# Queries' latent columns among the key products, the norm's shift added at the reload, the next weights split behind the queries: a change to a two-layer trunk kernel

## The chip, the cores and the metric

The kernel runs on one core of a Trainium2 chip. The metric is the time of one execution on the device in microseconds (us); several executions are timed and the median is taken. A smaller number is better. Times of the trace are counted from the start of its span.

## The reference

The program is a small trunk of two layers over 256 latent rows and 256 context rows of 1024 features, in float32. Layer 0 mixes with a bidirectional chunked mLSTM, layer 1 with multi-head latent attention; a gated ConvFFN follows each mixer. The change lies in layer 1's attention, which the reference computes like this (cut):

```python
def _mla_q(h, w_dq, q_norm, w_uq, ang):
    q = (_rms_norm(h @ w_dq, q_norm) @ w_uq).reshape(B, T, A_HEADS, A_DNOPE + A_DROPE)
    q_nope, q_rope = jnp.split(q, [A_DNOPE], axis=-1)
    return jnp.concatenate([q_nope, _axial_rope(q_rope, ang[0][:, None], ang[1][:, None])], -1)

def _mla_kv(h, w_dkv, kv_norm, w_ukv, ang):
    ckv, k_rope = jnp.split(h @ w_dkv, [A_KVLORA], axis=-1)
    k_rope = _axial_rope(k_rope, ang[0], ang[1])
    kv = (_rms_norm(ckv, kv_norm) @ w_ukv).reshape(B, T, A_HEADS, A_DNOPE + A_DV)
    ...

yl = _blocked_attend(ql, k_all, v_all).reshape(B, T, -1) @ w_out
x  = _layer_norm(ALPHA * x + ml[2] * yl, ln_g[i, 0], ln_b[i, 0])
```

There are 8 heads; keys and values are the 256 context rows and the 256 latent rows, queries are the latent rows alone. The residual `x` that goes into the last line is the output of layer 0's second norm: normalised rows times a gain `ln_g` plus a shift `ln_b` over the 1024 features.

## The kernel before, in words

**Precision.** Each float32 operand of a product is split into a high and a low part: ACT casts to the matmul type (high), DVE subtracts (low). A product is then three matmuls: high x high, high x low, low x high (`mm3`, lines 395 to 397). A tile with two parts is a "u" tile; there are 31 of them. Weights go through the class `Stream`: SP's queue loads a raw block of up to 1024 columns (line 299), ACT casts it (L334) and DVE subtracts (L337). The parts of a "wide" block go into two u tiles, those of others into one of three "w" tiles (`NB`). `use` splits ahead as far as `limit` allows, `pump(limit)` splits up to an index of the planned order without using anything. A raw block's buffer is loaded again when its split has been done.

**The order.** The kernel is written as a program for a scheduler that builds one in-order list for each engine: TensorE (PE), VectorE (DVE), ScalarE (ACT), GpSimd (POOL), and SP's queue. It may put an instruction ahead of others of the program if its operands and buffers allow it by its own account. `issue_after(i)` keeps what is issued under it behind the instruction `i`.

**Around the change**, in order of time (the function `mla`, line 1690 onwards):

- `dkv_mm`, and the four `dq` steps: latent columns of keys and values, and of the queries.
- `ln_x` (L1273), run in the background: it multiplies the layer-0 rows `z` by the gain (L1282), adds the shift (L1283) and stores them to DRAM as `x2d` (L1284, POOL's queue). Gain and shift rows (`gr`, `br`) are loaded by `bcast` (L1143).
- `rms` (L1574 to L1577) makes the normalised latent columns `cq` of the queries.
- `ukn(1)` (L1636): products `kn` of all 8 heads' keys for the latent rows, 48 matmuls of 256 columns.
- `cqT`: six PE transposes of `cq` (L1719), scaled and split (L1721, L1722).
- `qr`: the rotary parts of all queries (weights `uqr`), then `uv`: the values `v`; then rotation, scaling and split of `qr` into `qrs` (L1585 to L1587, L1747, L1748).
- `queries(i)`: the other part `qn` of the queries of heads 2i and 2i+1 (three weight blocks `uqn`, used from heads 0, 2 and 5 on), split at L1767 and L1768.
- `rotary(i)`: transposes `qrT` of two heads' rotary parts (L1776) and their copy (L1779).
- Then a loop over the heads h: transposes `PT` of the probabilities of head h-2 (L1810) with their split, `scores(h)` (products `s`, L1791 for the rotary part; maximum L1793; exp L1795; reciprocal L1796; multiply L1797 on the probabilities `P`), `attend(h-2)` (products `o`, split into `oT`). In it, `st.pump(ao + h)` splits weight blocks for what follows; `ao` is the index of the first `uqn` block, the eight `aout` blocks (output product) come three later, then the blocks of the next FFN (`fin1`).
- `res_load` (L1321) loads the residual rows from `x2d` into four tiles `xres` on POOL's queue; `bcast` loads the gate. `outmm("aout", ...)` makes the output product `y`, and `ln_rows` (L1148) the gated residual (L1157, L1158) and its norm.

Of the kernel before, what the change touches and what calls it, by code (L numbers as in the profile page):

```python
# [10 lines left out]
AF = mybir.ActivationFunctionType  # L11
ALU = mybir.AluOpType
# [15 lines left out]
H1 = 8  # L28
# [7 lines left out]
SUMS = 5  # L36

IDLE = 5

AHEAD = 8  # L40
QA, QB, QC = 2, 4, 6
# [324 lines left out]
class K:  # L366
# [866 lines left out]
    def ln_T4(self, zs, A, B, dst):  # L1233
# [6 lines left out]
        for t in range(2):  # L1240
# [5 lines left out]
            if not t:  # L1246
                for _ in range(IDLE):
                    pin(nc.tensor.matmul(idle, w[:, 0:128], w[:, 0:512], start=True, stop=True))
# [20 lines left out]
            if k % 2:  # L1269
                yield  # L1270

    def ln_x(self, ln, zs, dst):


        nc = self.nc
        g = self.bcast(self.a["ln_g"][ln:ln + 1, :], "gr")
        b = self.bcast(self.a["ln_b"][ln:ln + 1, :], "br")
        yield
        for t in range(2):
            for h in range(2):  # L1280
                c = slice(h * 512, (h + 1) * 512)
                nc.vector.tensor_tensor(zs[t][:, c], zs[t][:, c], g[h], op=ALU.mult)  # L1282
                nc.vector.tensor_tensor(zs[t][:, c], zs[t][:, c], b[h], op=ALU.add)  # L1283
                nc.gpsimd.dma_start(dst[t][:, c], zs[t][:, c])  # L1284
                yield

# [28 lines left out]
            r.append([(self.ps("y")[:, 0:b - a], slice(a, b)) for a, b in zip(cuts, cuts[1:])])  # L1315
        return r

    def res_load(self, src, t0):
        xs = []
        for t in range(2):  # L1320
            hs = []  # L1321
            for h in range(2):
                x = self.s2("xres")
                self.nc.gpsimd.dma_start(x, src[t0 + t][:, h * 512:(h + 1) * 512])
                hs.append(x)
            xs.append(hs)
        return xs
# [305 lines left out]
                nc.scalar.copy(self.krT[:, 0, cs], p)  # L1633
                nc.vector.tensor_sub(self.krT[0:64, 1, cs], p[0:64], self.krT[0:64, 0, cs])

    def ukn(self, g):  # L1636

        cs = slice(g * 256, (g + 1) * 256)
        for h in range(H1):
            w = self.wk[h // 4]  # L1640
            if h % 2 == 0:
                ps = self.ps("kn")
            hs = slice((h % 2) * 256, (h % 2 + 1) * 256)
            for k in range(2):
                c = slice((h % 4) * 256 + k * 128, (h % 4) * 256 + (k + 1) * 128)
                self.mm3(ps[:, hs], (w[0][:, c], w[1][:, c]), (self.ckT[k][:, 0, cs], self.ckT[k][:, 1, cs]),
                         k == 0, k == 1)
            if h % 2:
                for j in range(2):
                    u = self.kn[h - 1 + j]  # L1650
                    self.split(u[:, 0, cs], u[:, 1, cs], ps[:, j * 256:(j + 1) * 256])
# [36 lines left out]
    def mla(self, hl):  # L1688
        nc, st = self.nc, self.st
# [6 lines left out]
        for c in range(4):  # L1696
            w = st.use(("dq", 0, c))
            self.tick()
            for kk in range(2):
                k = 2 * c + kk  # L1700
# [8 lines left out]
        for t in range(2):  # L1709
            r = self.s2("cq")  # L1710
            self.rms(pss[t][:, 0:384], 384, r[:, 0:384])
            cq.append(r)
        self.ukn(1)
        g = self.smc("qng")
        cqT = []
        for k in range(3):
            pt = self.ps("cqT")
            for t in range(2):
                nc.tensor.transpose(pt[:, t * 128:(t + 1) * 128], cq[t][:, k * 128:(k + 1) * 128], self.ident)  # L1719
            u = self.hf("cqT")  # L1720
            nc.scalar.activation(u[:, 0], pt[:, 0:256], AF.Copy, scale=g[:, k:k + 1])  # L1721
            nc.vector.scalar_tensor_tensor(u[:, 1], pt[:, 0:256], g[:, k:k + 1], u[:, 0],  # L1722
                                           op0=ALU.mult, op1=ALU.subtract)
            cqT.append(u)
        pss = [self.ps("qr0"), self.ps("qr1")]
        for c in range(2):
            w = st.use(("uqr", 0, c))
            for kk in range(2 - c):
                k = 2 * c + kk
# [9 lines left out]
        scale = float((DN + DR) ** -0.5)  # L1739

        qr = []
        for t in range(2):
            r = self.s2("qr")
            self.rope_rows(r, pss[t], t, 512)
            u = self.pool.tile([128, H1, 2, 64], F32R, tag="u", name="qrs", bufs=NU)
# [8 lines left out]
        def queries(i):  # L1754

            ps = self.ps("qn")
            for h in (2 * i, 2 * i + 1):
                hs = slice((h % 2) * 256, (h % 2 + 1) * 256)
                for k in range(3):
                    b = h * 3 + k  # L1760
                    if b % 8 == 0:
                        wq[0] = st.use(("uqn", 0, b // 8))
                    c = slice((b % 8) * 128, (b % 8 + 1) * 128)
                    self.mm3(ps[:, hs], (wq[0][0][:, c], wq[0][1][:, c]), (cqT[k][:, 0], cqT[k][:, 1]),
                             k == 0, k == 2)
            u = self.u("qn")
            nc.scalar.activation(u[:, 0], ps, AF.Copy, scale=scale)  # L1767
            nc.vector.scalar_tensor_tensor(u[:, 1], ps, scale, u[:, 0], op0=ALU.mult, op1=ALU.subtract)  # L1768
            qn.append(u)

        def rotary(i):

            pt = self.ps("qrT")
            for j in range(2):
                for t in range(2):
                    nc.tensor.transpose(pt[:, j * 256 + t * 128:j * 256 + (t + 1) * 128],  # L1776
                                        qr[t][:, 2 * i + j].rearrange("p a b -> p (a b)").bitcast(F32), self.ident)
            u = self.pool.tile([128, 512], F32R, tag="s2", name="qrT", bufs=NS)
            nc.scalar.copy(u, pt)  # L1779
            qrT.append(u)  # L1780
# [3 lines left out]
        def scores(h):  # L1784
            Ps = []
            for t in range(2):
                ps = self.ps("s1")
                c = slice((h % 2) * 256 + t * 128, (h % 2) * 256 + (t + 1) * 128)
                self.mm3(ps, (qn[h // 2][:, 0, c], qn[h // 2][:, 1, c]), (kn[h][:, 0], kn[h][:, 1]), True, False)
                for x in range(2):  # L1790
                    nc.tensor.matmul(ps, qrT[h // 2][:, c], krT[:, x], start=False, stop=x == 1)  # L1791
                mx, sm = self.tiny(1, "mx"), self.tiny(1, "sm1")
                nc.vector.tensor_reduce(mx, ps, axis=AX.X, op=ALU.max, negate=True)  # L1793
                P = self.s2("P1")
                nc.scalar.activation(P, ps, AF.Exp, bias=mx, scale=1.0, accum_out=sm)  # L1795
                nc.vector.reciprocal(sm, sm)  # L1796
                nc.vector.tensor_scalar(P, P, sm, None, op0=ALU.mult)  # L1797
                Ps.append(P)
            return Ps
# [3 lines left out]
        def trans(h, Ps):  # L1803
            PT = []
            for i in range(2):
                pt = self.ps("PT1")
                for j in range(2):
                    s = 2 * i + j
                    for t in range(2):
                        nc.tensor.transpose(pt[:, j * 256 + t * 128:j * 256 + (t + 1) * 128],  # L1810
                                            Ps[t][:, s * 128:(s + 1) * 128], self.ident)
                u = self.u("PT1")
                self.split(u[:, 0], u[:, 1], pt)
                PT.append(u)
            return PT
# [11 lines left out]
            oc = slice((h % 2) * 256, (h % 2 + 1) * 256)  # L1827
            self.split(oT[-1][:, 0, oc], oT[-1][:, 1, oc], ps[:, 0:256])

        ao = st.nu  # L1830
        Ps, PTs = {}, {}
        queries(0)
        queries(1)
        rotary(0)
        for h in range(H1 + 1):
            if 1 <= h < H1:
                st.pump(ao + h)
            if h >= 2:
                PTs[h - 2] = trans(h - 2, Ps.pop(h - 2))
            if h < H1:  # L1840
                Ps[h] = scores(h)
            if h < 6 and h % 2 == 1:
                rotary(h // 2 + 1)
            if h < 2:
                queries(h + 2)
            if h >= 2:
                attend(h - 2, PTs.pop(h - 2))
        yield oT
# [6 lines left out]
def build(tc, off, a, out):  # L1855
    es = ExitStack()
    with es:
        k = K(tc, es, off, a)
        nc = k.nc
# [44 lines left out]
        xr = k.res_load(tokr, 0)  # L1904
# [19 lines left out]
        xr = k.res_load(tokr, 2)  # L1924
# [20 lines left out]
        x2d = k.dr.tile([2, 128, D], F32, name="x2d")  # L1945
# [5 lines left out]
        def mid(g, zs, stats, first=None):  # L1951
            if g is None:
                st.limit = kv0 + PA
                k.rope_load()
                k.mla_ctx(hc)
                return
            return norm1(g, zs, stats, first)

        def norm1(g, zs, stats, first):
            A, B = k.ln_mod_cols(1, 1, 0, 1 - g)  # L1960
            if first is not None:
                first()
                hlu.extend([k.u("hl") for _ in range(4)])
            yield from k.z_norm(zs, stats)
            yield from k.ln_T(zs, A, B, hl if g else hc, g == 1, False)
            if g:
                k.late.append(k.ln_x(1, zs, [x2d[0], x2d[1]]))
        k.w_fout0(x1d, mid)
        hc = hcu = None
        k.tick(1)  # L1970
# [11 lines left out]
        hl = hlu = None  # L1982
        o1 = lambda i: (oT[i // 2][:, 0, (i % 2) * 256:(i % 2 + 1) * 256],
                        oT[i // 2][:, 1, (i % 2) * 256:(i % 2 + 1) * 256])
        xr = k.res_load(x2d, 0)
        gate = k.bcast(k.gd[1, 2][0:1, :], "gate")
        pl = k.acc4(True)
        k.outmm("aout", range(8 - TAIL["aout"]), o1, pl, 0, 8, 1)
# [21 lines left out]
        xr = k.res_load(x3d, 0)  # L2010
        gate = k.bcast(k.gd[1, 5][0:1, :], "gate")
        gr = k.bcast(a["ln_g"][3:4, :], "gr")
        br = k.bcast(a["ln_b"][3:4, :], "br")
# [23 lines left out]
```

## Time and profile before

| what | value |
|---|---|
| median of 3 runs | 1361.63 us (1359.55 to 1362.25) |
| the profiled execution's own time | 1359.2 us |
| its span | 1357.4 us |
| granted TensorE clock, mean | 0.999 |
| instructions on PE / DVE / ACT / POOL | 6663 / 1731 / 1236 / 216 |
| HBM read, written | 263.03 MB, 33.46 MB |

The profile comes from one execution that took 1359.2 us; it shows 1357.4 us of it as its span, and the rest lies around it. In a row of a timeline the first number is the start in us, the second the duration in us, then engine, line and operation, what is written and read, the shape and a count; in brackets at the end the idle time of the engine before it and who ended it. In a list of waits the numbers are us in total, times, and the longest. Rows of the chain of waits give start, length, engine and line. PE's matmuls overlap each other: a row may last 0.39 us while the next one starts 0.23 us after it.

### The profile page before, as it was taken

The page shows a single profiled execution, that of the slowest core. Times are in us where ns is not written, and L with a number is a line of the kernel's source. Part 1 is how long each engine was busy: PE and PEld are TensorE (multiplying, and loading weights), DVE is VectorE, ACT ScalarE, POOL GpSimd, SP SyncE. Part 2 cuts the span into 40 slices and gives each one's busy share as a digit, 9 for nine tenths or more (in the row PEclk, how much of TensorE's full clock was granted, in tenths as well). Part 3 has the DMA queues.
Part 4 walks back from the last instruction along what each step waited for, and adds up shares of the span by engine and source line. Part 5 has one row for each costly group of instructions (what it writes and reads, how often), then busy time and mean ns, then how long its engine had stood idle before and what let it go on. Part 6 is the DMA issues. An engine that isn't in the chain of part 4 may idle for free.

```text
span 1357.4 us, 18736 instructions
## 1 busy us (share of the span) xinstructions
PE 1342.4 (99%) x6663; PEld 1120.6 (83%) x6663; DVE 1056.4 (78%) x1731; ACT 711.9 (52%) x1236; POOL 122.1 (9%) x216
## 2 busy tenths in 40 slices
PE   9999999999999999999999999999999999999997
PEld 6777888888888888888898888888888888888886
DVE  4787756677688697897979878667898889888873
ACT  4764544445734545464644334334557767466660
POOL 0122000011101011030001000000001000000100
PEclk9999999999999999999999999999999999999999
DMA  9887848789676374785727877646997436366750
GB/s 368 315 271 269 294 162 245 235 289 304 215 250 194 98 246 142 239 297 190 232 92 250 295 234 236 213 148 215 309 279 220 140 102 223 104 192 188 256 194 31
DMA packets 92078, 297.73 MB, mean 219 GB/s; under 512 B 12073, under 2 KB 16425, under 8 KB 91985
## 3 DMA queue, kind: packets, MB, share of 16 engines
q1 hardware_dynamic: 62848, 218.65, 48.7%
q0 software_dynamic: 17472, 57.57, 13.6%
q10 hardware_dynamic: 11664, 20.32, 4.2%
q8 instruction: 52, 0.85, 0.3%
q14 instruction: 42, 0.34, 0.1%
HBM read 263.03 MB, written 33.46 MB: 218 GB/s over the span
## 4 chain that ended last, share of the span: by engine, by line
PE 93%; DMA 3%; DVE 2%; ACT 1%; issue 1%; ACTq 0%; SPq 0%; DVEq 0%
PE fin L1374 8%; PE y L396 6%; PE y L397 6%; PE y L395 6%; PE fin L395 6%; PE fin L396 6%; PE fin L397 6%; PE tok L395 6%; PE tok L396 6%; PE tok L397 6%; PE qk L395 4%; PE qk L397 4%; PE qk L396 4%; DMA adaw<-in_ada 2%; PE up L395 2%; PE up L397 1%
## 5 line engine op out<-in xcount | busy, mean ns | idle before, releaser
L337 DVE TENSOR_TENSOR w<-raw,w 128x1024 fp32r<-128x1024 f32 (+2 forms) x286 | 343.8, 1204 | 140.0 <-ACT w L334 139.2
L334 ACT CAST w<-raw 128x1024 fp32r<-128x1024 f32 (+2 forms) x286 | 297.2, 1039 | 290.8 <-PE tok L397 78.4
L500 DVE SCALAR_TENSOR_TENSOR junk<-ar,bc 128x1024 f32<-128x1024 f32 x128 | 156.2, 1220 | 4.0 <-ACT bc L542 1.4
L396 PE MATMUL fin<-h,w 128*128 128x512 f32 (+1 forms) x376 | 141.2, 376 | 0.0
L397 PE MATMUL fin<-h,w 128*128 128x512 f32 (+1 forms) x376 | 140.9, 375 | 0.0
L395 PE MATMUL fin<-h,w 128*128 128x512 f32 (+1 forms) x376 | 140.8, 376 | 0.1
L1374 PE MATMUL fin<-h,w 128*128 128x256 f32 (+1 forms) x640 | 111.9, 337 | 0.0
L1374 PEld LDWEIGHTS fin<-h,w 128*128 128x128 f32 x640 | 98.3, 190 | 13.4
L395 PE MATMUL qk<-xc,w 128*128 128x512 f32 x256 | 100.6, 393 | 0.0
L397 PE MATMUL qk<-xc,w 128*128 128x512 f32 x256 | 99.9, 390 | 0.0
L396 PE MATMUL qk<-xc,w 128*128 128x512 f32 x256 | 99.8, 390 | 0.0
L396 PEld LDWEIGHTS fin<-h,w 128*128 128x128 f32 x376 | 70.8, 188 | 12.9 <-DVE h L1228 0.2
L397 PEld LDWEIGHTS fin<-h,w 128*128 128x128 f32 x376 | 70.8, 188 | 12.9
L395 PEld LDWEIGHTS fin<-h,w 128*128 128x128 f32 x376 | 70.5, 188 | 13.1 <-ACT h L1227 0.3
L397 PEld LDWEIGHTS qk<-xc,w 128*128 128x128 f32 x256 | 48.1, 188 | 9.8
L396 PEld LDWEIGHTS qk<-xc,w 128*128 128x128 f32 x256 | 48.1, 188 | 9.7
L395 PEld LDWEIGHTS qk<-xc,w 128*128 128x128 f32 x256 | 48.1, 188 | 9.7
L395 PE MATMUL tok<-w,hT 128*128 128x512 f32 x128 | 49.9, 390 | 0.0
L397 PE MATMUL tok<-w,hT 128*128 128x512 f32 x128 | 49.8, 389 | 0.0
L396 PE MATMUL tok<-w,hT 128*128 128x512 f32 x128 | 49.8, 389 | 0.0
L681 ACT ACTIVATE fg<-fg 128x512 f32<-128x512 f32 (+1 forms) x44 | 23.2, 527 | 46.1 <-DVE fg L679 39.9
L337 DVE TENSOR_TENSOR wu<-raw,wu 128x1024 fp32r<-128x1024 f32 (+1 forms) x37 | 43.7, 1204 | 4.1 <-ACT wu L334 3.9
(470 smaller groups left out, 3142.3 us busy)
## 6 DMA issues: line engine op xcount, KB each, us to landing
raw<-in_ws SPq DMA_DIRECT2D x282, 512.0 KB, 4.6
ar<-in_adaT SPq DMA_DIRECT2D x80, 512.0 KB, 4.6
adaw<-in_ada SPq DMA_DIRECT2D x16, 512.0 KB, 8.0
t2d<-raw ACTq DMA_DIRECT2D x13, 512.0 KB, 4.8
raw<-t2d SPq DMA_DIRECT2D x13, 512.0 KB, 6.6
raw<-in_ws POOLq DMA_DIRECT2D x13, 512.0 KB, 7.9
zr<-fd ACTq DMA_DIRECT2D x33, 128.0 KB, 4.6
xmd<-xr POOLq DMA_DIRECT2D x16, 256.0 KB, 4.8
```

Source lines behind the costliest of these rows:

```text
L334: k.nc.scalar.copy(h[:, :cols], src)
L337: k.nc.vector.tensor_sub(l[:, :cols], src, h[:, :cols])
L395: mm(out, w[0], x[0], start=start, stop=False, skip_group_check=on)
L396: mm(out, w[0], x[1], start=False, stop=False, skip_group_check=on)
L397: mm(out, w[1], x[0], start=False, stop=stop, skip_group_check=on)
L500: nc.vector.scalar_tensor_tensor(o, w, 1.0, self.bc[j], op0=ALU.mult, op1=ALU.mult, accum_out=col[:, k, j:j + 1])
L681: nc.scalar.activation(tmp[:, :n], tmp[:, :n], AF.Silu)
L1374: nc.tensor.matmul(ps[:, :n] if x else ps, w[x][:, c], hT(k)[0] if x else both(k), start=i == 0, stop=i == 15)
```

## The change

1. `ln_x` gets a parameter `shift`. For the rows of layer 0's second norm it is False: neither are the shift's rows loaded nor are they added by DVE; what is stored is rows times gain. At the reload, `res_load` gets the shift's row as `base`: it first fills each residual tile with the shift (a transfer that repeats one row over all partitions), and a second transfer of POOL's queue adds the stored rows to it.
2. `ukn` takes a range of heads. The key products of heads 0 to 5 (`QH = 6`) come before the transposes of `cq`, those of heads 6 and 7 behind them.
3. In the attention, `limit` is set to the third `uqn` block before the queries, so that it isn't split by them; it is split by a pump behind the split of the second pair of queries (`issue_after` both of its instructions). The pumps in the loop stand behind the split of the last queries in the same way, and their base is the third `uqn` block instead of the first.

```diff
+QH = 6
...
-    def ln_x(self, ln, zs, dst):
+    def ln_x(self, ln, zs, dst, shift=True):
...
-        b = self.bcast(self.a["ln_b"][ln:ln + 1, :], "br")
+        if shift:
+            b = self.bcast(self.a["ln_b"][ln:ln + 1, :], "br")
...
-                nc.vector.tensor_tensor(zs[t][:, c], zs[t][:, c], b[h], op=ALU.add)
+                if shift:
+                    nc.vector.tensor_tensor(zs[t][:, c], zs[t][:, c], b[h], op=ALU.add)
...
-    def res_load(self, src, t0):
+    def res_load(self, src, t0, base=None):
...
-                self.nc.gpsimd.dma_start(x, src[t0 + t][:, h * 512:(h + 1) * 512])
+                c = slice(h * 512, (h + 1) * 512)
+                if base is not None:
+                    self.nc.gpsimd.dma_start(x, base[:, c].to_broadcast([128, 512]))
+                    self.nc.gpsimd.dma_start(x, src[t0 + t][:, c], accum_op=ALU.add)
+                else:
+                    self.nc.gpsimd.dma_start(x, src[t0 + t][:, c])
...
-    def ukn(self, g):
+    def ukn(self, g, heads=range(H1)):
...
-        for h in range(H1):
+        for h in heads:
...
-        self.ukn(1)
+        self.ukn(1, range(QH))
...
             cqT.append(u)
+        self.ukn(1, range(QH, H1))
...
-            nc.scalar.activation(u[:, 0], ps, AF.Copy, scale=scale)
-            nc.vector.scalar_tensor_tensor(u[:, 1], ps, scale, u[:, 0], op0=ALU.mult, op1=ALU.subtract)
             qn.append(u)
+            return (nc.scalar.activation(u[:, 0], ps, AF.Copy, scale=scale),
+                    nc.vector.scalar_tensor_tensor(u[:, 1], ps, scale, u[:, 0], op0=ALU.mult, op1=ALU.subtract))
...
-        ao = st.nu
         Ps, PTs = {}, {}
+        q2 = [x[0] for x in st.order].index(("uqn", 0, 2))
+        st.limit = q2
         queries(0)
-        queries(1)
+        last = queries(1)
+        with self.tc.issue_after(last[0].ins), self.tc.issue_after(last[1].ins):
+            st.pump(q2 + 1)
+        ao = q2
         rotary(0)
         for h in range(H1 + 1):
             if 1 <= h < H1:
-                st.pump(ao + h)
+                with self.tc.issue_after(last[0].ins), self.tc.issue_after(last[1].ins):
+                    st.pump(ao + h)
...
             if h < 2:
-                queries(h + 2)
+                last = queries(h + 2)
...
-                k.late.append(k.ln_x(1, zs, [x2d[0], x2d[1]]))
+                k.late.append(k.ln_x(1, zs, [x2d[0], x2d[1]], False))
...
-        xr = k.res_load(x2d, 0)
+        xr = k.res_load(x2d, 0, a["ln_b"][1:2, :])
```

## The prediction

> **What bounds the kernel now.** I read the page first, then a table of stretches around the edited code, then the timelines of TensorE (PE), VectorE (DVE) and ScalarE (ACT) in it.
>
> ```profile
> span 1357.4 us, 18736 instructions
> PE 1342.4 (99%) x6663; PEld 1120.6 (83%) x6663; DVE 1056.4 (78%) x1731; ACT 711.9 (52%) x1236; POOL 122.1 (9%) x216
> ...
> PE 93%; DMA 3%; DVE 2%; ACT 1%; issue 1%; ACTq 0%; SPq 0%; DVEq 0%
> ```
>
> PE is the bound: it makes 93% of the chain that ended last. An edit that leaves PE's instructions as they are can only win what PE idles. The built order of the changed kernel differs from the old one only between the key products of the latent rows (about 1072 us) and the norm after the attention's output product (about 1161 us). SyncE's queue (SP) keeps its order. So I look there.
>
> ```profile
> 1093.75:1103.75 10.00, 10.00 (x65) 8.84 (x66) 7.06 (x17) 6.20 (x13) 0.00 (x0) 1.00 0.31 104
> 1103.75:1118.05 14.30, 14.30 (x96) 12.92 (x95) 12.41 (x26) 9.29 (x23) 1.65 (x3) 1.00 0.18 57
> 1118.05:1139.82 21.77, 21.04 (x139) 18.53 (x137) 18.94 (x38) 15.15 (x34) 3.53 (x7) 1.00 0.46 145
> ...
> sum 88.48, PE 86.89 PEld 77.03 DVE 78.43 ACT 56.90 POOL 7.65; mean PE 17.38 PEld 15.41 DVE 15.69 ACT 11.38 POOL 1.53
> ```
>
> Columns: stretch, length, then busy us of PE, weight load, DVE, ACT, POOL, the granted clock, DMA share, GB/s. The sum covers 1072.04 to 1160.52 in five stretches. PE idles 88.48 - 86.89 = 1.59 us there. The places:
>
> ```profile
> 1078.78 0.50 PE L395 MATMUL qr<-w,cqT 128*128 128x512 f32 x1 [0.18 <-ACT cqT L1721]
> ...
> 1092.81 0.27 PE L1776 MATMUL qrT<-ident,qrs 128*128 128x128 f32 x1
> 1093.75 0.51 PE L395 MATMUL s<-kn,qn 128*128 128x512 f32 x1 [0.67 <-ACT qn L1767]
> 1094.10 0.40 PE L396 MATMUL s<-kn,qn 128*128 128x512 f32 x1
> ...
> 1132.69 0.39 PE L396 MATMUL o<-PT,v 128*128 128x256 f32 x1 [0.37 <-DVE PT L401]
> ...
> 1139.82 0.35 PE L395 MATMUL o<-PT,v 128*128 128x256 f32 x1 [0.21 <-DVE oT L401]
> ```
>
> A stall costs more than its idle number, since the pipeline empties. From the 0.11 us that a transpose takes of PE, the second row's successor starts 0.94 - 0.11 = 0.83 us late, and the next row 0.35 us later instead of 0.23: 0.95 us for an idle of 0.67. With some 0.15 us of refill at each of six places, **all that this stretch can give is about 2.5 us**.
>
> **The change part by part.**
>
> (a) Six of eight heads' key products ahead of the transposes of the queries' latent columns, two behind; and the four adds of the norm's shift gone from DVE.
>
> ```profile
> 1072.04 0.28 PE L395 MATMUL kn<-ckT,wu 128*128 128x256 f32 x1
> ...
> 1077.78 0.82 PE L1719 MATMUL cqT<-ident,cq 128*128 128x128 f32 x6
> ```
> ```profile
> 1073.98 1.88 DVE L1283 TENSOR_TENSOR z<-z,br 128x512 f32<-128x512 f32 x3
> 1075.78 0.21 DVE L1576 RECIPROCAL rs<-rs 128x1 f32<-128x1 f32 x2
> ```
> ```profile
> 1075.97 1.05 ACT L1577 ACTIVATE cq<-dq,rs 128x384 f32<-128x384 f32 x2 [0.49 <-DVE rs L1576]
> ...
> 1078.25 1.21 ACT L1721 ACTIVATE cqT<-cqT,sm 128x256 fp32r<-128x256 f32 x3
> ```
>
> 48 key products take 1072.04 to 1077.78, 0.12 us each. Now the transposes follow the 36th, at 1076.36, and 12 products (1.43 us) stand between them and qr. The old wait at 1078.78 (0.33 us with the refill) has that cover. But cq was ready only at 1077.0, because DVE's reciprocals stood behind three adds (1.88 us). Without the adds they come at about 1074.0 and cq at about 1075.4, one us before the transposes. If the adds were still there, the transposes would wait 0.65 us; so the two edits need each other. Gain 0.35 us, between 0 and 0.45.
>
> (b) The split of the last query weight and of the first output weight (aout 0) put behind the queries' own splits.
>
> ```profile
> 1091.64 1.05 ACT L334 CAST w<-raw 128x1024 fp32r<-128x1024 f32 x1 [1.75 <-issue]
> ...
> 1093.12 1.06 ACT L1767 ACTIVATE qn<-qn 128x512 fp32r<-128x512 f32 x2
> ```
>
> That cast waits for a weight buffer that PE is still reading (w holds three), and the rotary split and the query split qn queue behind it on ACT. In the new order both qrs and both qn come first. The first qn can then follow PE's 18th query product, near 1090.8, and is done on ACT and DVE before PE asks for it. The wait of 0.95 us goes. What is late next is the rotary transposes' copy, which now stands behind the query weight's cast (1.05 us): the rotary part of head 0's scores waits about 0.35 us. The old order lost some 0.25 us in the same place:
>
> ```profile
> PEld s L1791 <- ACT qrT L1779: 0.6, 2, 0.3
> ```
>
> (two waits of the weight load for this copy, 0.3 us each; the other is at 1125.9). Net gain 0.85 us, between 0.4 and 0.95.
>
> (c) The pump's base moves from the first query weight to the third (`ao = q2`), so aout splits come two heads earlier. In DVE's built order ten weight splits now lie between head 0's first maximum and the last head's transposed split; before there were four. This is the cost side.
>
> ```profile
> 1145.90 3.49 DVE L337 TENSOR_TENSOR wu<-raw,wu 128x1024 fp32r<-128x1024 f32 x3
> ...
> 1111.60 0.69 DVE L1793 TENSOR_REDUCE mx<-s 128x1 f32<-128x512 f32 x1 [0.25 <-PE s L1791]
> ```
> ```profile
> 1112.33 0.69 ACT L1795 ACTIVATE P<-s,mx 128x512 f32<-128x512 f32 x1 [0.16 <-DVE mx L1793]
> ...
> 1113.01 0.57 ACT L1779 CAST qrT<-qrT 128x512 fp32r<-128x512 f32 x1
> ...
> 1113.92 1.07 ACT L400 CAST PT<-PT 128x512 fp32r<-128x512 f32 x2
> ```
> ```profile
> 1108.37 0.87 PE PT L1810 x8
> 1109.25 0.23 PE s L395
> ...
> 1111.57 0.44 PE qrT L1776 x4
> ...
> 1118.05 0.87 PE PT L1810 x8
> ```
>
> PE needs 1118.05 - 1108.37 = 9.68 us for two heads, and had no stall there because no split stood in those heads. A split takes 1.13 us of DVE ((3.49 - 1.22)/2) and about 1 us of ACT. DVE was busy 7.06 + 12.41 + 18.94 = 38.41 of 46.07 us from 1093.75 to 1139.82; six more splits make 45.2. So they fit, barely, and order decides. In heads 3 and 5 the new order puts one exp of the newest scores before the split of the previous head's transposes on ACT. From the start of those scores: first half 5 x 0.23, maximum 0.69, exp 0.68 until the next ACT instruction, cast 0.57, four hand-overs of about 0.04: 3.2 us. PE has 10 x 0.23 + 0.44 = 2.8 us of work until it asks: 0.45 us in head 3, 0.55 in head 5. In head 7 a weight split stands in front of the maxima on DVE, and PE waits twice, 0.6 and 0.55 us. Together 2.15 us. Against it go the old stalls from late splits at 1125.9 (0.3), 1132.69 (0.5) and 1139.82 (0.45): 1.25 us. Net loss 0.9 us. Bounds: a gain of 1.25 if nothing waits, a loss as in rival 1.
>
> (d) The shift loaded into the residual tiles and the stored rows added by accumulating transfers.
>
> ```profile
> 1112.11 0.55 POOL L1324 DMA_DIRECT2D xres<-x2d  x1 [28.65 <-PE qrT L1776]
> ...
> 1121.78 0.55 POOL L1143 DMA_DIRECT2D gate<-gd  x1 [1.58 <-PE qrT L1776]
> ```
> ```profile
> br<-in_ln_b POOLq DMA_DIRECT2D x4, 256.0 KB, 4.1
> ```
> ```profile
> raw<-in_ws POOLq DMA_DIRECT2D x13, 512.0 KB, 7.9
> ```
> ```profile
> 1112.40 0.49 DVE L1797 TENSOR_SCALAR P<-P,sm 128x512 f32<-128x512 f32 x1
> ...
> 1151.04 0.69 DVE L1158 SCALAR_TENSOR_TENSOR z<-xres,z 128x512 f32<-128x512 f32 x1
> ```
>
> POOL's queue loses two loads of br and gains four. The four base loads take the places of the old residual loads, as they wait for the same kind of buffer (released by PE's transposes), all before the gate's row at 1121.78. Four accumulating ones follow in the queue once a base has landed (4.1 us), near 1125, and land between 4.1 us later and 7.9 us (a transfer of twice the size that accumulates): by 1133. The gate rows behind them, held up by some 4 us, land by about 1131. Both are used at 1149 to 1151: 16 us of cover, cost nothing. The stored rows that they read come from DVE products that stand ahead of the query chain. If that cover went, each us late would delay the norm at the end of the product.
>
> The row at 1112.40 is such a multiply under a POOL issue (1112.11 to 1112.66); it lasts 0.49 us like the others, so the issues cost DVE nothing here. By the Trainium skill, "SBUF — State Buffer", section "Who interferes with whom", such a multiply and GpSimd's writing of descriptors lock each other out of a shared port; by that rule two more issues would add at most 2 x 0.55 = 1.1 us to the sum. This one row does not agree with it.
>
> **The sum**: -0.35 - 0.85 + 0.9 + 0 = -0.3 us. The profiled execution took 1359.2 us, so 1358.9 on its terms; the runs shown have a median of 1361.63 (1359.55 to 1362.25), 2.4 us above it, so **1361.3 us** on theirs, with 1360.0 to 1363.0 as this case's own range.
>
> **The rivals.**
>
> 1. *DVE becomes the bound in the attention* (slower). The old idle of DVE there, 46.07 - 38.41 = 7.7 us, is partly not free:
>
> ```profile
> DVE mx L1793 <- PE s L1791: 2.7, 4, 1.2
> DVE w L337 <- ACT w L334: 1.8, 1, 1.8
> DVE sm L1796 <- ACT P L1795: 1.7, 6, 0.5
> ```
>
> The waits for scores and for exp (2.7 + 1.7, with small ones some 5 us) are latency that a split can fill only if it stands just there. If all 5 stay, the stretch takes 45.2 + 5.0 = 50.2 instead of 46.07: +4.1, less the 1.2 of (a) and (b): +2.9, 1364.5 us. It decides from 4.8 us of unfilled idle (which makes +2.7). Against it: the old head pairs overlapped such waits freely. For it: ten splits in seven heads, and 45.2 of 46.07.
>
> 2. *Every stall goes* (faster). If the hand-overs of (c) fit PE's order after all, -2.5 us: 1359.1 us. For it: aout 1 to 5 split early means no split late, and the load that fed the split at 1138 starts earlier. Against it: the order on ACT in heads 3 and 5.
>
> 3. *A transfer is late*: the gate or a residual tile arrives after 1151. Every us is paid; it needs 16 us of delay. A wait of 2 us gives 1363.3 us.
>
> 4. *The port's lock*: two POOL issues block DVE for 1.1 us where DVE is full: 1362.4 us. One row speaks against it.
>
> That the change does not do what it says is excluded for the order, which stands in the built kernel.
>
> **How the numbers follow.** A measurement of this kernel tells about 0.2%, 2.7 us, from no change. Forecast 0.46, rival 1 0.32, rival 2 0.14, rival 3 0.03, rival 4 0.05. Rival 2's centre (-2.5) lies just inside the edge: half of it, 0.07, and 0.03 of the forecast's case make 0.10 faster. Rival 1's centre (+2.9) lies just beyond it: two thirds, 0.21, with 0.05 of the forecast's case (its loss in (c) too small) and 0.02 of rival 3, make 0.28 slower. The rest, 0.62, is the same. The range takes in rival 2 and rival 1 to 1364.7: 1358.9 to 1364.7.
>
> **What would show it.** (a): no wait of qr for cqT. (b): the first score product directly behind the rotary transposes, at about 1092.5 on the old clock. (c): PE waiting for ACT or DVE PT at the o products of heads 1, 3 and 5, 0.4 to 0.6 us each; if these waits are absent rival 2 is right, if every head has them and DVE is busy over 95% from head 1 on, rival 1. (d): no wait for a DMA at the residual's add (L1158 before). I would be wrong altogether if anything before 1072 or after 1165 us moved, since nothing there is edited.

## The result, and the profile after

The changed kernel is **slower**, by 0.3%: 1364.44 us (median of 11 runs, 1362.18 to 1368.43) against 1360.52 us for the kernel before on the same chip (11 runs, 1359.51 to 1362.84). The ratio is 1.0032 with a 95% interval of 1.0024 to 1.0040. The forecast was no change, 1361.3 us: 0.3 us under a median of 1361.63 us from three runs. Over the 11 runs that median is 1360.52 us, so the change itself, +3.9 us where -0.3 was forecast, was missed by more than the time was. The time lies in the stated range, 1358.9 to 1364.7 us, but only at the end that rival 1 put there. The profiled execution took 1363.23 us, so its terms are some 1.2 us below the median.

Lines have moved: +1 up to L1272, +8 or +9 in the attention. The split of a weight is now L335 (ACT) and L338 (DVE), the matmuls of a product L396 to L398, the split of `PT` and `oT` L401 and L402, the score maximum L1802, the exp L1804, the multiply on `P` L1806, the transposes `PT` L1819.

From the page of the changed kernel: the span, the engines' busy time, and the chain that ended last by engine.

```profile
span 1361.5 us, 18740 instructions
...
PE 1344.3 (99%) x6663; PEld 1122.3 (82%) x6663; DVE 1054.5 (77%) x1727; ACT 710.9 (52%) x1236; POOL 124.5 (9%) x218
...
PE 93%; DMA 3%; DVE 1%; ACT 1%; issue 0%; ACTq 0%; SPq 0%; DVEq 0%
```

The page tells almost nothing: DVE lost the four adds, POOL gained two transfers, and the span is 4.1 us longer with the same chain. So I cut the stretch in two at the first product `o` (the one with the probabilities): from the first `kn` to the first `o`, and from there to the first transpose `zT` of the norm's result. Columns of the table of stretches: stretch, length, busy us of PE, weight load, DVE, ACT, POOL, granted clock, DMA share, GB/s. First the kernel before, then the changed one.

```profile
1072.04:1106.78 34.74, 33.88 (x215) 30.03 (x215) 30.11 (x57) 21.41 (x46) 2.18 (x4) 1.00 0.44 142
1106.78:1160.52 53.74, 53.01 (x331) 47.00 (x329) 48.31 (x87) 35.49 (x66) 5.47 (x10) 1.00 0.55 187
```
```profile
1072.74:1106.16 33.42, 33.42 (x215) 30.16 (x215) 26.81 (x51) 21.56 (x46) 2.17 (x4) 1.00 0.40 135
1106.16:1164.42 58.26, 54.97 (x331) 48.17 (x330) 49.66 (x89) 35.84 (x66) 9.30 (x14) 0.97 0.67 199
```

The front stretch has become 1.32 us shorter, and PE has no idle time left in it. The back stretch has become 4.52 us longer. Together that is +3.20 us. The rest of the span's 4.1 us lies ahead of 1072 (0.70 us) and behind 1164 us; the start of the first `kn`, with the same code ahead of it, scatters from 1071.82 to 1075.09 us over the profiles of this study.

TensorE's timeline of the changed kernel shows where:

```profile
1079.12 0.40 PE L396 MATMUL qr<-w,cqT 128*128 128x512 f32 x1
...
1093.38 0.48 PE L396 MATMUL s<-kn,qn 128*128 128x512 f32 x1
...
1111.98 0.39 PE L396 MATMUL o<-PT,v 128*128 128x256 f32 x1 [0.47 <-ACT PT L401]
...
1122.41 0.39 PE L396 MATMUL o<-PT,v 128*128 128x256 f32 x1 [0.48 <-ACT PT L401]
...
1131.31 0.63 PE L1800 MATMUL s<-krT,qrT 128*128 128x512 f32 x2
1134.02 0.55 PE L396 MATMUL o<-PT,v 128*128 128x256 f32 x1 [2.08 <-ACT PT L401]
...
1135.25 0.58 PE L397 MATMUL o<-PT,v 128*128 128x256 f32 x1 [0.26 <-DVE PT L402]
```

`qr` and the first `s` start without a wait: both gains of the front are there. The two waits of 0.47 and 0.48 us (heads 3 and 5) are the ones that the prediction named. The wait of 2.08 us behind the last head's scores is not. The chain of waits leads from it straight back to a transfer:

```profile
1121.47 1.14 DVE wu L338
...
1122.63 7.05 DMA raw<-in_ws
...
1129.71 1.06 ACT w L335
...
1130.79 1.23 DVE w L338
...
1132.09 0.60 DVE mx L1802
...
1132.71 0.78 ACT P L1804 x2
1133.49 0.97 ACT PT L401 x2
```

Read it upwards: PE waits for ACT's split of the transposes, this stands on ACT behind an exp, the exp needs a maximum, the maximum stands on DVE behind the split of a weight (`w`, 1130.79), and that split waited for its load, which started as soon as the third wide `aout` block had been split and took 7.05 us. ACT's timeline shows the queue at this point:

```profile
1125.90 1.10 ACT L401 CAST PT<-PT 128x512 fp32r<-128x512 f32 x2
1129.71 1.05 ACT L335 CAST w<-raw 128x1024 fp32r<-128x1024 f32 x1 [2.71 <-DMA raw<-in_ws]
1130.66 0.68 ACT L1804 ACTIVATE P<-s,mx 128x512 f32<-128x512 f32 x1
```

ACT stands idle for 2.71 us in front of the cast of a narrow block; in the built order it is the first narrow block of the next FFN, `fin1(2,0)`. The program uses it only after the attention. The scheduler put it here, ahead of the last head's exp, because by its own account the block's data and buffer are ready. Why did the load take 7 us? The transfers issued from 1110 to 1140 us, with their median time to landing, in the changed kernel and then in the kernel before:

```profile
q0 software_dynamic: 1136, 2.88, 43.8%
...
raw<-in_ws SPq DMA_DIRECT2D x7, 512.0 KB, 6.9
xres<-in_ln_b POOLq DMA_DIRECT2D x4, 256.0 KB, 4.4
xres<-x2d POOLq DMA_DIRECT2D x4, 256.0 KB, 8.4
gate<-gd POOLq DMA_DIRECT2D x2, 256.0 KB, 9.0
```
```profile
q0 software_dynamic: 720, 2.36, 24.1%
...
raw<-in_ws SPq DMA_DIRECT2D x4, 512.0 KB, 4.2
xres<-x2d POOLq DMA_DIRECT2D x4, 256.0 KB, 3.0
gate<-gd POOLq DMA_DIRECT2D x2, 256.0 KB, 4.2
```

The residual rows (`xres<-x2d`) now take 8.4 us to land instead of 3.0, the gate behind them 9.0 instead of 4.2, and the weight loads beside them are slow as well. The medians of these loads rest on few: the trace has the landing of three of the seven here (7.05 and 6.9 us for those that started at 1122.6 and 1126.0 us, 3.6 for one at 1132.0) and of two of the four in the kernel before (4.9 and 3.4). POOL's queue (q0) occupies the engines for 43.8% of these 30 us instead of 24.1%, for 2.88 MB instead of 2.36: 73 engine-us for each MB (0.438 x 16 x 30 / 2.88) against 49.

### The profile page after: what moved, and what is told of

It is laid out like the page before. It is cut to its first block, busy times and chain, and to the rows that moved or that the text cites. A ratio compares the mean times of both kernels' runs of the same rounds, so it can differ in the third digit from the quotient of the medians.

```text
span 1361.5 us, 18740 instructions
## 1 busy us (share of the span) xinstructions
PE 1344.3 (99%) x6663; PEld 1122.3 (82%) x6663; DVE 1054.5 (77%) x1727; ACT 710.9 (52%) x1236; POOL 124.5 (9%) x218
## 4 chain that ended last, share of the span: by engine, by line
PE 93%; DMA 3%; DVE 1%; ACT 1%; issue 0%; ACTq 0%; SPq 0%; DVEq 0%
PE fin L1382 8%; PE y L397 7%; PE y L398 7%; PE y L396 7%; PE fin L396 6%; PE fin L397 6%; PE fin L398 6%; PE tok L396 6%; PE tok L397 6%; PE tok L398 6%; PE qk L396 4%; PE qk L398 4%; PE qk L397 4%; DMA adaw<-in_ada 2%; PE up L396 2%; PE up L397 1%
## 5 line engine op out<-in xcount | busy, mean ns | idle before, releaser
L338 DVE TENSOR_TENSOR w<-raw,w 128x1024 fp32r<-128x1024 f32 (+2 forms) x286 | 343.7, 1204 | 140.4 <-ACT w L335 136.2
L335 ACT CAST w<-raw 128x1024 fp32r<-128x1024 f32 (+2 forms) x286 | 296.4, 1037 | 285.9 <-PE tok L398 74.2
L398 PE MATMUL fin<-h,w 128*128 128x512 f32 (+1 forms) x376 | 140.9, 375 | 0.0
L396 PE MATMUL fin<-h,w 128*128 128x512 f32 (+1 forms) x376 | 140.8, 376 | 0.1
L396 PE MATMUL qk<-xc,w 128*128 128x512 f32 x256 | 100.6, 393 | 0.0
L398 PE MATMUL qk<-xc,w 128*128 128x512 f32 x256 | 99.9, 390 | 0.0
L396 PEld LDWEIGHTS fin<-h,w 128*128 128x128 f32 x376 | 70.6, 188 | 13.2 <-ACT h L1228 0.3
L398 PEld LDWEIGHTS fin<-h,w 128*128 128x128 f32 x376 | 70.8, 188 | 12.8
L398 PEld LDWEIGHTS qk<-xc,w 128*128 128x128 f32 x256 | 48.1, 188 | 9.9
L396 PEld LDWEIGHTS qk<-xc,w 128*128 128x128 f32 x256 | 48.1, 188 | 9.7
L396 PE MATMUL tok<-w,hT 128*128 128x512 f32 x128 | 49.9, 390 | 0.0
L398 PE MATMUL tok<-w,hT 128*128 128x512 f32 x128 | 49.8, 389 | 0.0
L338 DVE TENSOR_TENSOR wu<-raw,wu 128x1024 fp32r<-128x1024 f32 (+1 forms) x37 | 43.7, 1203 | 3.6 <-ACT wu L335 3.3
```

Of the source, the lines that this page charges most:

```text
L335: k.nc.scalar.copy(h[:, :cols], src)
L338: k.nc.vector.tensor_sub(l[:, :cols], src, h[:, :cols])
L396: mm(out, w[0], x[0], start=start, stop=False, skip_group_check=on)
L398: mm(out, w[1], x[0], start=False, stop=stop, skip_group_check=on)
```

## The experiments

**Theory T1**: the loss needs two parts of the change together. The accumulating transfers slow the load of `fin1(2,0)`, and the earlier splits of part 3 put that block's split ahead of the last head's softmax. **T2**: the place of the splits alone is late, whatever the load takes. **T3**: VectorE is the bound, the prediction's rival 1. **T4**: VectorE and GpSimd lock each other out, its rival 4. All times beside a run of the kernel before on the same chip; the last two columns are the two stretches in one profiled execution of each.

| kernel | median us | before | ratio (95%) | front | back |
|---|---|---|---|---|---|
| before | | | | 34.74 | 53.74 |
| e4: key order alone (part 2) | 1358.86 | 1359.68 | 0.9991 (0.9982 to 1.0000) | 33.59 | 53.55 |
| e2: shift at the reload alone (part 1) | 1358.97 | 1359.68 | 0.9993 (0.9984 to 1.0002) | 34.03 | 53.56 |
| e3: splits alone (part 3) | 1360.75 | 1359.68 | 1.0003 (0.9994 to 1.0012) | 33.86 | 55.06 |
| e1: parts 2 and 3 | 1360.29 | 1359.68 | 1.0003 (0.9994 to 1.0011) | 33.77 | 55.17 |
| e5: parts 1 and 2 | 1357.91 | 1359.94 | 0.9987 (0.9978 to 0.9996) | 33.29 | 53.55 |
| e8: all, pump's base as before | 1358.37 | 1359.94 | 0.9991 (0.9982 to 1.0000) | 33.43 | 53.56 |
| e6: all, second transfer overwrites | 1359.97 | 1359.94 | 1.0000 (0.9991 to 1.0009) | 33.42 | 55.04 |
| e7: all, `fin1` splits held back | 1360.39 | 1359.94 | 1.0008 (0.9999 to 1.0017) | 33.42 | 55.28 |
| the changed kernel | 1364.44 | 1360.52 | 1.0032 (1.0024 to 1.0040) | 33.42 | 58.26 |
| e10: the changed kernel again | 1365.27 | 1360.45 | 1.0039 (1.0025 to 1.0053) | 33.43 | 59.63 |
| e9: all, PE kept busy in the wait | 1365.10 | 1360.45 | 1.0036 (1.0023 to 1.0048) | 33.42 | 58.31 |
| e11: parts 1 and 2 again | 1358.98 | 1360.45 | 0.9987 (0.9978 to 0.9996) | 33.29 | 53.57 |

The back stretch has three values: 53.6 us without the early splits, 55.0 to 55.3 with them, 58.3 to 59.6 with them and the accumulating transfers ahead of a split that waits.

### One part away, one part alone

**e1**, without part 1:

```diff
-                k.late.append(k.ln_x(1, zs, [x2d[0], x2d[1]], False))
+                k.late.append(k.ln_x(1, zs, [x2d[0], x2d[1]]))
-        xr = k.res_load(x2d, 0, a["ln_b"][1:2, :])
+        xr = k.res_load(x2d, 0)
```

> The changed kernel without the accumulating transfers: the shift is added by VectorE again and the rows come back by one plain transfer each; the key products' order and the splits behind the queries stay as changed. Theory T1 (the ten transfers of the reload slow the first weight load of the block behind the attention output, raw 7.05 us against 4.2 to 4.9 us before, and its split stands ahead of the last head's softmax on ScalarE and VectorE): the raw load takes 4.2 to 5 us, TensorE's wait of 2.08 us at the last head's attention product goes or falls below 0.5 us, time 1361 to 1362.3 us, that is 2 to 3.5 us under the changed kernel. Rival T2 (the new place of the splits alone is late, with any load time): the wait stays over 1.5 us, 1363.5 to 1364.5 us. Rival T3 (VectorE is the bound): 0.4 to 1.5 us slower than the changed kernel, since VectorE has the shift's adds again: 1364.8 to 1366 us.

Measured: 0.6 us over the kernel before; T1's case, a little below its range. The chain of waits of e1 has the same load in the same place, but shorter:

```profile
1123.61 4.99 DMA raw<-in_ws
...
1128.63 1.06 ACT w L335
```

ACT waits 0.65 us for it, and TensorE's waits at the last head are nothing and 0.56 us (T1 said below 0.5). So with the same order of splits, the load's time alone decides about the 2 us: T2 falls. T3 falls as the main cause too: VectorE has the same splits in the same places here, and in the changed kernel it is itself idle for 2.12 us where the time is lost (the row is shown with the rivals below).

**e2**, part 1 alone, **e3**, part 3 alone, and **e4**, part 2 alone (the same hunks of the change, put on the kernel before):

> The kernel before with the accumulating transfers alone; order of key products and splits as before. T1: the weight load that stood at 1132 us in the kernel before comes after most of the slow transfers, so the loss appears only if it is still slowed: 1360.5 to 1362.5 us, with the stall wherever a raw load of over 5 us is seen between 1110 and 1135 us. T2: nothing of the loss, 1360.0 to 1360.8 us. A port shared by GpSimd's transfers and VectorE: VectorE's instructions between 1112 and 1133 us get longer, about 1361.6 us.

> The kernel before with the splits behind the queries alone. T1: no slowed load, so what the prediction's terms say for this part alone, 1360.0 to 1361.5 us, and no wait over 1 us at the last head's attention product. T2: nearly the whole loss, 1363 to 1364.5 us, with a wait of some 2 us at the last head. T3: over 1363 us with VectorE over 95% busy from the second head on.

> The kernel before with the latent columns of the queries among the key products alone. All theories: the wait of the queries' rotary product for them goes (0.35 us in the prediction's sum), 1360.0 to 1360.5 us; a rise would speak for a later start of the weights behind.

Measured, by the medians: e2 gains 0.7 us, e3 loses about 1, e4 gains 0.8. The interval of each of these ratios takes in 1.0000, so the argument rests on the stretches and the waits and not on these totals. In e2 the transfers are slow too (the residual rows' median to landing is 7.6 us between 1115 and 1135 us), but no split that the last head needs waits for a load behind them: its back stretch is 53.56 us, 0.2 under the kernel before. Its time, 1358.97 us, lies 1.5 us under T1's range. T2 expected no loss in e2 either, so e2 does not part these two; it speaks against T4. e3 parts them: it has neither a wait over 0.48 us at the last head nor the loss that T2 asked for. e4 gains more than the 0.35 us expected: its front stretch is 1.15 us shorter, since the wait of the first score has gone too.

### Which property of the transfers

**e6** lets the second transfer overwrite the shift instead of adding to it. This leaves the shift out of the result.

```diff
-                    self.nc.gpsimd.dma_start(x, src[t0 + t][:, c], accum_op=ALU.add)
+                    self.nc.gpsimd.dma_start(x, src[t0 + t][:, c])
```

> The changed kernel, with the second transfer of each residual tile written over the shift and not added to it, so the shift is left out of the result; the number of transfers, their bytes, their order and everything else stay. T1a (accumulating is what is slow): the second transfers land in 3 to 4.5 us as plain ones do (8.4 us in the changed kernel), the raw load in under 5.5 us (7.05), the wait at the last head goes below 0.6 us: 1360 to 1361.5 us. T1b (it is the four more transfers with their 1 MB that share the engines): the second transfers still take over 6 us, the wait stays above 1.5 us, within 0.7 us of the changed kernel (1363.5 to 1364.8 us).

Measured: 1359.97 us, level with the kernel before. The same number of transfers with the same bytes, issued from 1110 to 1140 us in e6:

```profile
raw<-in_ws SPq DMA_DIRECT2D x7, 512.0 KB, 4.5
...
xres<-x2d POOLq DMA_DIRECT2D x4, 256.0 KB, 4.4
```

And the last head's wait, 2.08 us in the changed kernel:

```profile
1132.51 0.39 PE L397 MATMUL o<-PT,v 128*128 128x256 f32 x1 [0.42 <-DVE PT L402]
```

The second transfer lands in 4.4 us instead of 8.4, and the two weight loads that follow it take 4.5 and 5.5 us instead of 7.05 and 6.9. Four more transfers cost little; **that they accumulate is what is slow** (T1a). The back stretches differ by 58.26 - 55.04 = 3.22 us.

### Which half can be mended in the order

**e7** keeps the transfers, and holds the splits of the first narrow `fin1` blocks behind the last head's split of `PT` on both engines.

```diff
-                self.split(u[:, 0], u[:, 1], pt)
+                self.held = (nc.scalar.copy(u[:, 0], pt), nc.vector.tensor_sub(u[:, 1], pt, u[:, 0]))
...
-        st.pump(fi + QC)
+        with tc.issue_after(k.held[0].ins), tc.issue_after(k.held[1].ins):
+            st.pump(fi + QC)
```

> The changed kernel, with the splits of the feed-forward's first narrow blocks kept behind the last head's transposed splits on ScalarE and VectorE; transfers as changed. T1: the load still takes 6 to 8 us, but only its split waits for it, nothing of the last head: TensorE's wait of 2.08 us there goes below 0.6 us, 1360 to 1361.8 us. If it stays above 1363 us, the load was not what made the last head late, or another split (the sixth output block's) takes its place.

Measured: 1360.39 us, in the range. The loads started at 1122 to 1127 us are as slow as in the changed kernel (time to landing, lowest, median and highest), but TensorE waits 0.91 us at the last head and no longer 2.08:

```profile
DMA to landing us min/median/max: 7.2/7.5/7.8
```
```profile
1132.78 0.39 PE L396 MATMUL o<-PT,v 128*128 128x256 f32 x1 [0.91 <-ACT PT L1822]
```

So a slow load costs next to nothing here as long as nothing of the attention stands behind its split: the back stretch is 55.28 us, against 55.04 in e6. My bound for the wait (0.6 us) was missed: the sixth `aout` block's split has moved up to the softmax (ACT 1130.36 us) in the place of the narrow one.

**e8** puts the pump's base back (`ao = q2 - 2`); the split of the last query block stays behind the queries.

> The changed kernel with the pump's base put back to the first query weight: the last query weight and the first output weight still stand behind the queries, the other output weights are split as late as in the kernel before. T1: the narrow block's split stands behind the last head's softmax again, so no loss, near the kernel with shift and key order alone: 1 to 2.2 us under the kernel before. If the splits behind the queries cost something of their own: 0 to 1 us above that one.

Measured: 1.6 us under the kernel before, as the first reading had it. In the built order `fin1(2,0)` is then split behind the last head's probabilities. So part 3's first half (the block behind the queries) costs nothing, but front and back are also no better than in e5, which doesn't have it: 33.43 and 53.56 against 33.29 and 53.55 us.

### The clock behind the wait

In the changed kernel TensorE's granted clock falls behind the 2.08 us. Three of the one-us stretches, and one of the second profile (e10), in the table of stretches (the seventh number is the clock, DMA share and GB/s follow):

```profile
1133.00:1134.00 1.00, 0.00 (x0) 0.00 (x0) 1.00 (x3) 1.00 (x4) 0.19 (x1) 1.00 0.91 238
1134.00:1135.00 1.00, 0.98 (x3) 0.57 (x3) 1.00 (x3) 1.00 (x2) 0.00 (x0) 0.54 0.95 373
...
1136.00:1137.00 1.00, 1.00 (x7) 1.00 (x6) 1.00 (x3) 0.00 (x0) 0.00 (x0) 0.50 0.82 291
```
```profile
1138.00:1139.00 1.00, 1.00 (x7) 1.00 (x6) 1.00 (x2) 0.24 (x1) 0.00 (x0) 0.50 0.75 270
```

**e9** fills the wait with eight products that nobody reads.

```diff
+                if h == H1 - 1 and t == 1:
+                    idle = self.ps("idle")
+                    for _ in range(8):
+                        self.tc.keep_in_program_order(nc.tensor.matmul(idle, kn[h][:, 0, 0:128], kn[h][:, 0], start=True, stop=True))
```

> The changed kernel with eight products whose result nobody reads, put on TensorE behind the last head's scores, where it waits 2.08 us for the transposes' split. They take about 8 x 0.23 = 1.84 us, so the wait itself stays (the split comes no earlier), but TensorE is no longer idle. In the changed kernel the granted clock is 0.50 to 0.54 from 1134 to 1137 us, right behind the idle 2.08 us, and the products there start 0.21 us apart instead of 0.12: 1.2 us of its loss by that reading. If the low clock follows from the idle time: the clock stays 1.00 there and the time falls by 0.8 to 1.4 us against the changed kernel, to 1362.8 to 1363.8 us. If the low clock has another cause: still 0.5 behind the wait, within 0.4 us of the changed kernel.

> The changed kernel once more, beside the other two. It should be 3 to 5 us over the kernel before, with a raw load of some 7 us ahead of the last head, a wait of some 2 us there and the granted clock at 0.5 behind it. If the profile shows the wait and no low clock, or the load under 5.5 us, the accounting from one profile was chance.

Measured: half a hit. The clock stays at full speed in the profile, so the low clock does follow from the idle time; the mean granted clock of the five runs, 0.997 to 0.998 against 0.996 to 0.997 in e10, fits. But the time is 1365.10 us, within 0.2 us of the changed kernel run beside it. One stretch of e9, and two rows of its PE timeline behind the wait:

```profile
1134.00:1135.00 1.00, 0.29 (x2) 0.29 (x3) 1.00 (x4) 0.85 (x1) 0.00 (x0) 1.00 0.91 365
```
```profile
1134.71 0.38 PE L397 MATMUL o<-PT,v 128*128 128x256 f32 x1 [0.85 <-DVE PT L402]
...
1137.86 0.38 PE L396 MATMUL o<-PT,v 128*128 128x256 f32 x1 [0.71 <-ACT PT L401]
```

The third busy number is VectorE: 1.00 of 1.00 us. Behind the late load VectorE works off what has piled up, and a faster TensorE only waits for it (0.85 and 0.71 us here, 0.26 in the changed kernel). So the 1.2 us that I had put down to the clock are not shown to be a term of their own. The orders of ACT and DVE behind the wait differ a little in e9, so what a full clock is worth in the unchanged order stays open.

e10 repeats the loss: a load of 7.91 us, a wait of 2.93 us, the clock at 0.50 and a back stretch of 59.63 us.

```profile
1123.31 7.91 DMA raw<-in_ws
```
```profile
1135.55 0.39 PE L396 MATMUL o<-PT,v 128*128 128x256 f32 x1 [2.93 <-ACT PT L401]
```

The low clock doesn't begin at the end of this wait: the mean is still 1.00 from 1136.5 to 1137 us and 0.62 from 1137 to 1138. More load time, more loss, in these two profiles: 0.86 us more on the load, 1.37 us more in the stretch.

### The version that beats both

**e5** takes the accumulating transfers and the key order, and leaves the splits where they were (e4's hunk on e2); **e11** is the same kernel again.

> The kernel before with the accumulating transfers and the new order of the key products; the splits stay where they were. The four kernels of the first job took, against the kernel before: shift alone -0.7 us, key order alone -0.8, splits alone +1.1, key order and splits without the shift +0.6 (medians). Theory T1 (the loss of the changed kernel needs both: a weight load slowed by the reload's transfers, and its split standing ahead of the last head's softmax): no loss here, the two gains add up as far as they don't end the same wait: 1.0 to 2.2 us under the kernel before, no wait over 0.6 us at the last head. Rival: the transfers slow a load that is waited for in this order too, in the last weights of the attention output: within 0.5 us of the kernel before or above it.

> The kernel before with the accumulating transfers and the key order, once more: 1.5 to 2.6 us under the kernel before and 5 to 7 us under the changed one, no wait over 0.6 us at the last head. If it comes out within 0.7 us of the kernel before, the gain of the first measurement was chance.

Measured: 2.0 and 1.5 us under the kernel before, both times with a ratio of 0.9987 (0.9978 to 0.9996); 6.3 us under the changed kernel in the same job. Its two stretches:

```profile
1071.82:1105.11 33.29, 33.29 (x216) 30.01 (x215) 28.31 (x53) 21.86 (x46) 2.17 (x4) 1.00 0.44 146
1105.11:1158.66 53.55, 53.04 (x331) 47.01 (x329) 48.43 (x87) 35.46 (x66) 9.41 (x14) 1.00 0.68 207
```

The front has no idle time, and the back is the one of the kernel before. POOL's transfers are as busy as in the changed kernel (9.41 us) and cost nothing here.

## Why the prediction was wrong

**Steps (a) and (b), right in sum.** They were to gain 0.35 + 0.85 = 1.20 us; the front stretch gained 1.32. Both signs asked for are there. The credit was wrong, though. I gave 0.85 us to the split of the query block behind the queries. e2 and e4 do not have that edit, and in both the first score follows the rotary transposes without a wait. With the key order alone or the shift alone, the scheduler by itself puts the first `qn` ahead of that weight's split; why it does so is not shown. In e5 two rows show it:

```profile
1090.18 0.60 ACT L1777 ACTIVATE qn<-qn 128x512 fp32r<-128x512 f32 x1 [0.48 <-PE qn L398]
1090.93 1.05 ACT L335 CAST w<-raw 128x1024 fp32r<-128x1024 f32 x1 [0.15 <-PE qn L398]
```

Three parts end one wait, and any one of them is enough (in e3 the first score doesn't wait either). "The two edits need each other" for (a) was wrong too: in e4, with the adds, the transposes wait so little that all of the front's best gain (34.74 - 33.29) but 0.30 us is there.

**Step (c), right in mechanism, a little small.** Forecast: 2.15 us of new waits less 1.25 of old ones, +0.9 us. Heads 3 and 5 wait as said (0.47 and 0.48 us). With a load that is on time, the back stretch is longer by 1.30 us (e6), 1.32 (e3) and 1.43 (e1). In e6 the first `o` starts 0.63 us late in each of these heads, the two places at the last head 0.25 and 0.58 us: 2.09, less 1.30 for the old ones counted the same way, 0.8 us. The other 0.5 us is in no wait that the traces name.

**Step (d), the one that failed.** Its term in the sum was 0. It said that the accumulating transfers "land between 4.1 us later and 7.9 us", with "16 us of cover, cost nothing". Their landing was sized a little low (8.4 us; the gate behind them landed by about 1134 us, not 1131), and for their own users the cover held. The residual's add and the multiply by the gate start without waiting for a transfer:

```profile
1150.37 0.68 DVE L1158 TENSOR_TENSOR z<-y,gate 128x512 f32<-128x512 f32 x1
1151.09 0.69 DVE L1159 SCALAR_TENSOR_TENSOR z<-xres,z 128x512 f32<-128x512 f32 x1
```

What I did not ask is what else these transfers share. I looked for who waits for them, not for who travels beside them. SP's weight load did, took 7.05 us instead of 4.99, and by step (c) its split now stood ahead of the last head's softmax. (c) priced that split as busy time (1.13 us of VectorE), with its data taken as landed. The two steps were costed one by one; their product, 58.26 - 55.04 = 3.22 us, was in neither. By measured sizes the sum is -1.32 + 1.30 + 3.22 = +3.20 us. As all three are differences of the same two stretches, it has to meet their change; it shows where the loss lies, from one profile each. e10 loses 4.6 us in the same two stretches, and the medians lie 3.9 us apart.

By the Trainium skill, "DMA: Bandwidth & Descriptors", section "Rules for kernel authors", transfers issued by SP, ACT and GpSimd run on the same 16 engines and interleave, and an accumulating one reads its destination before it writes. The loads fit the first: 7.05 and 6.9 us beside accumulating transfers, 4.5 and 5.5 beside plain ones (e6). That the destination is read first is in no row here.

**The rivals.** Rival 1 gave the right time (1364.5 us) by the wrong mechanism. Where the 2 us are lost, VectorE is idle, waiting for ACT's cast:

```profile
1130.79 1.23 DVE L338 TENSOR_TENSOR w<-raw,w 128x1024 fp32r<-128x1024 f32 x1 [2.12 <-ACT w L335]
```

In a mild form it is true all the same: in e6, where no load is late, VectorE is busy without a gap over the last two heads, which fits (c)'s 1.3 us.

```profile
1121.88:1134.70 12.82, 12.32 (x81) 10.85 (x82) 12.82 (x25) 10.48 (x20) 2.26 (x4) 1.00 0.84 277
```

Rival 2 (every stall goes) is refuted by the waits of heads 3 and 5, rival 3 (a late gate or residual) by the rows at 1150 and 1151. Rival 4 (the port's lock) is not seen: the multiply under POOL's issue of three transfers lasts 0.48 us as elsewhere, and e2 has these issues without a loss.

```profile
1119.91 2.78 POOL L1330 DMA_DIRECT2D xres<-x2d  x3
```
```profile
1120.99 0.48 DVE P L1806
```

## What to carry to other kernels

Ask of a transfer that is "covered" not only when its own user needs it, but which other loads are under way beside it, and whose split or copy stands in an in-order queue ahead of critical work. An early split was not free here even with its data landed (1.3 us of the back stretch), and it cost 3.2 us more where its load was late; a scheduler that takes the load's time from its own account will put it in front of work that could run. Where several edits end the same wait, try each alone: here two of the three gave the whole gain; the third added nothing to it, and its early `aout` splits cost 1.3 us.

## What the runs showed of the hardware

- An accumulating transfer of 256 KB into SBUF took 7.5 to 8.8 us to land (medians of four, in the eight profiles that have them), a plain one of the same shape, number and place 4.4 us, and one in the kernel before 3.0 us. Weight loads of 512 KB that started within some 6 us behind the accumulating ones and whose landing the trace has took 6.8 to 7.9 us (the changed kernel, e7, e9, e10), the same loads beside plain ones 4.5 to 5.5 (e6) and 3.7 to 5.0 (e1).
- TensorE's granted clock fell to 0.50 for some 3.5 us behind 2.08 us of idle time, and stayed at 1.00 behind 0.91 us (e7) and when the same wait was filled with products (e9). In e10, with 2.93 us of idle time and 0.62 more, it fell only some 1.7 us after TensorE had started again. By the Trainium skill, "TensorE: Matmul & The Clock Gate", section "Part 1: The HAM clock gate", the half clock comes after an idle window of about 3.4 us. Here 2.08 us were enough; the measurement decides.
- The changed kernel's runs scatter more than those of the kernel before (6.3 us from lowest to highest against 3.3, 11 runs each). That a wait which ends with a transfer brings the transfer's own scatter into the time is likely (7.05 us in one profile, 7.91 in the other), but two profiles do not show it.
